# A hand-ordered opening and w_out sample rows by raw weights, in a layer of a hybrid attention encoder

## The chip, the cores and the metric

The kernel runs on one core of a Trainium2 chip. A core has five engines with a queue of instructions each: TensorE (PE, matrix products and transposes, results in PSUM), VectorE (DVE), ScalarE (ACT), GpSimd (POOL) and SyncE (SP, which here only issues DMA transfers). PEld is the loading of PE's stationary operand. An engine runs its instructions in the order in which they were put down; semaphores tie the engines together. The metric is the device time of one execution in microseconds, and the median over several executions is compared.

## The reference

One layer (DEPTH = 1) for two groups of rows that share the weights: 1024 prompt rows and 32 sample rows, with D_MODEL = 1024. All data are float32.

```python
ada = silu(c) @ w_ada + b_ada            # six vectors of 1024 per group
h   = rms_norm(x, g_pre_mix) * (1 + scale1) + shift1
p   = h @ w_in                           # 4256 columns: q latent, kv latent, rope key,
                                         # stick-breaking q, k, v, gate A, gate B
# branch A: latent attention, branch B: stick-breaking attention
merged = sigmoid(g_a) * (o_a @ w_proj_a) + sigmoid(g_b) * (o_b @ w_proj_b)
x  = x + gate1 * rms_norm(merged @ w_out, g_post_mix)
h2 = rms_norm(x, g_pre_ffn) * (1 + scale2) + shift2
x  = x + gate2 * rms_norm(conv_ffn(h2), g_post_ffn)
```

The change touches the first lines (ada for shift1 and scale1, the norm, the first columns of `p`) and the sample rows of `merged @ w_out`.

## The kernel before

A float32 product is made of three matmuls in a faster type: each operand is split into a high part, which is the value rounded by ScalarE (`hi`, line 68), and a low part, the difference, which VectorE makes (`lo`, line 71). `mm3` (lines 75 to 77) adds high x high, low x high and high x low in PSUM. Activations lie transposed, with the model's columns in the 128 partitions (eight blocks k = 0 to 7) and the 1056 rows (1024 prompt, 32 sample) along the free axis. PSUM has eight banks of 512 float32 columns, in rings by tag: `s` three, `mm` two, `tr` two, `pv` one. Most engines' orders come from a scheduler that goes by the order of the program text and by estimated durations. Blocks under `manual_schedule` keep the order of the text on the engines that they name.

**The opening** is `stage_h` (line 372). `ada_prep` makes silu(c), turned. `ada_half(hf)` (line 276) fetches eight chunks of `w_ada`, each 128 rows by the half `hf` of the columns of shift1 and of scale1 (512 KB), and adds their products with `cT`; the sum is copied (line 290), turned by two transposes (line 293), and given its bias (line 296) and the norm's gain (`gain`, line 272). Half 0 serves blocks k = 0 to 3, half 1 blocks 4 to 7. A row tile of 128 prompt rows is loaded, squared and summed by ScalarE (line 116), scaled by its rstd from GpSimd (lines 108, 109) on VectorE (line 385). `norm_T` (line 302) transposes it in PE (line 320) and lets ScalarE read PSUM, with scale and shift of ada in the same activation (line 326); so a turned tile stays in PSUM until ada's half is known. VectorE then makes the high part (line 329, or ScalarE for rows 512 on) and the low part (line 330). Rows 512 on also stay in `fq` as float32, for sums that a later product scheme needs.

SP issues in the opening: four row tiles, eight chunks, one `w_in` tile, four row tiles, a second `w_in` tile, eight chunks.

**`stage_qkv`** (line 443) then multiplies three column tiles of `w_in` of 128 columns by `mtile` (line 415): q pair 0 (line 660), k pair 0 (line 673), and a latent tile (line 678). Each takes three blocks of 352 rows, eight k and three matmuls, 72 in all. The k tile is transposed back and stored (line 485). Then pairs of column tiles follow by a scheme with seven products instead of eight (`pair`, line 596); it needs sums of the activations T1 to T4, made by `sums` (line 564) from `fq` and the split rows on VectorE and ScalarE, and sums of weights (lines 608 to 613), which are split in their turn (`half`).

**`stage_merge`** (line 2067) goes over eight blocks m of merged columns: a `w_proj_a` tile is loaded into the ring `wr` of two buffers (line 1910) and split, its 36 matmuls are gated, and the merged block is split (`mh`, `ml`). A row block of `w_out` is loaded into the same ring (line 2119) and split. `natural` (line 1988) multiplies the merged blocks with `w_out` in groups: m = 0 and 1 after the products of m = 2, m = 2 and 3 in two parts at m = 4 and 6, the rest at the end. The sample rows go by `natural_s` (line 2020): 32 columns as stationary operand, the high and then the low part of `w_out` streamed as float32, four quarters of 256 columns side by side. It is called for two, four and two blocks with an eviction each time (line 2032 adds).

Of the kernel before, what the change touches and what calls it, by code (L numbers as in the profile page):

```python
# [44 lines left out]
class K:  # L45
# [224 lines left out]
    def gain(self, out, v, g0, k0=0, n=8):  # L270
        k = slice(k0, k0 + n)
        self.nc.vector.scalar_tensor_tensor(
            out[:, k], self.adaT[:, v, k], 1.0, self.gvT[:, g0 + k0 : g0 + k0 + n].unsqueeze(2).broadcast_to([P, n, 2]),
            ALU.add, ALU.mult)

    def ada_half(self, hf, wp, tp):

        nc, a = self.nc, self.a
        acc = self.tl(tp, [P, 256], F32, f"ada{hf}")
        ps = self.bank("s")  # L280
        for k in range(KT):

            last = hf == 1 and k >= KT - 2
            w = self.tl(*((self.W, [P, 1024]) if last else (wp, [P, 2 * 512])), F32, "wr").rearrange("p (v n) -> p v n", v=2)
            nc.sync.dma_start(w, a["w_ada"][0, k * P : (k + 1) * P].rearrange("p (v h n) -> p v h n", v=6, h=2)[:, 0:2, hf])
            for j in range(4):
                c = (j % 2) * 256
                nc.tensor.matmul(ps[32 * j : 32 * j + 32, :256], self.cT[:, k], w[:, j // 2, c : c + 256],
                                 start=k == 0, stop=k == KT - 1)
        nc.vector.tensor_copy(acc, ps[:, :256])  # L290
        tr = self.bank("s")
        for c in range(2):
            nc.tensor.transpose(tr[:, c * P : c * P + P], acc[:, c * P : c * P + P], self.idt)
        for c in range(2):
            k = slice(4 * hf + c, 4 * hf + 4, 2)
            nc.vector.tensor_tensor(self.adaT[:, 0:2, k],
                                    tr[:, c * P : c * P + P].rearrange("p (v j r) -> p v j r", v=2, j=2)[:, :, :, 0:2],
                                    self.bT[:, :, k].unsqueeze(3).broadcast_to([P, 2, 2, 2]), ALU.add)
        self.gain(self.g1, 1, 0, 4 * hf, 4)


    def norm_T(self, t0, xs, g, sv, tp, k0=0, k1=KT):


        nc = self.nc
        if t0 < 8:
            n = len(xs) * P
            m = 512 // n
            c = slice(t0 * P, t0 * P + n)
            for k in range(k0, k1, m):  # L310
                tr = self.bank("tr")
                if t0:
                    f = self.fq[:, k : k + m, :n]
                else:
                    f = self.tl(tp, [P, 512], F32, "hf").rearrange("p (k c) -> p k c", k=m)
                for e in range(m):
                    kc = slice((k + e) * P, (k + e) * P + P)
                    for j, x in enumerate(xs):
                        o = e * n + j * P
                        nc.tensor.transpose(tr[:, o : o + P], x[:, kc], self.idt)  # L320
                h, l = self.Hht[:, k : k + m, c], self.Hlt[:, k : k + m, c]

                both = t0 == 4 and k0 == 0
                for e in range(m):
                    for x in (f, h) if both else (f,):
                        nc.scalar.activation(x[:, e], tr[:, e * n : e * n + n], AF.Identity,
                                             bias=self.adaT[:, sv, k + e, 0:1], scale=g[:, k + e, 0:1])
                if not both:
                    nc.vector.tensor_copy(h, f)
                nc.vector.tensor_tensor(l, f, h.bitcast(F32), ALU.subtract)  # L330
        else:
            tr = self.bank("tr")
            for c in range(2):
                nc.tensor.transpose(tr[:, c * P : c * P + P], xs[0][:, c * P : c * P + P], self.idt)
            f = self.fq[:, :, 512:]
            for k in range(k0, k1):
                j, c = k // 2, k % 2
                nc.scalar.activation(f[:, k], tr[:, c * P + 32 * j : c * P + 32 * j + 32],
                                     AF.Identity, bias=self.adaT[:, sv, k, 1:2], scale=g[:, k, 1:2])
            f, h, l = (x[:, k0:k1] for x in (f, self.Hht[:, :, TP:T], self.Hlt[:, :, TP:T]))  # L340
            nc.vector.tensor_copy(h, f)
            self.lo(l, f, h)
# [10 lines left out]
    def rstd_s(self, f, tp):  # L353
# [5 lines left out]
        ps = self.bank("tr")  # L359
# [12 lines left out]
    def stage_h(self):  # L372
        nc = self.nc
        self.new_H()
        a = self.a
        self.Fq = self.tc.alloc_tile_pool(name="fq", bufs=1, reuse_waits="tile")
        self.fq = self.Fq.tile([P, KT, TP - 512 + TS], F32, name="fq")
        with self.tc.tile_pool(name="st_h", bufs=2, reuse_waits="tile") as tp, self.tc.tile_pool(name="wada", bufs=8, reuse_waits="tile") as wp:
            self.ada_prep(tp)
            xts = []  # L380

            def load(t):
                x = self.tl(wp, [P, D], F32, "x")
                nc.sync.dma_start(x, a["x_prompt"][0, t * P : (t + 1) * P])
                nc.vector.tensor_scalar(x, x, self.rstd(self.sumsq(x, P, tp, "jk0", 1024), D, P), None, ALU.mult)
                xts.append(x)

            def norm(t, hf):
                self.norm_T(t, xts[t : t + 4] if t < 8 else [xs], self.g1, 0, tp, 4 * hf, 4 * hf + 4)

            for t in range(4):
                load(t)
            self.ada_half(0, wp, tp)
            norm(0, 0)
            w = [self.w_in_tile(672)]
            mk = self.tl(tp, [P, 272], F32, "mk")
            nc.gpsimd.dma_start(mk, a["k_mask"][:, P:])
            nc.vector.tensor_copy(self.msk, mk)
            for t in range(4, 8):
                load(t)  # L400
            w.append(self.w_in_tile(672 + 512))
            self.in_w = w
            norm(4, 0)
            xs = self.tl(tp, [P, 256], F32, "xs")
            self.quarters(xs, a["x_sample"][0], nc.gpsimd)
            nc.gpsimd.dma_start(self.sel, a["k_sel"])
            self.ada_half(1, wp, tp)
            nc.vector.tensor_scalar(xs, xs, self.rstd_s(xs, tp), None, ALU.mult)
            norm(0, 1)
            norm(8, 0)  # L410
            norm(4, 1)
            norm(8, 1)
# [30 lines left out]
    def stage_qkv(self):  # L443
# [6 lines left out]
        T4, T3, T1, T2 = ([Tp.tile([P, 4, HC], F32R, name=self.nm("T")) for _ in range(2)] for _ in range(4))  # L450
# [208 lines left out]
        wh, wl = self.w_in_tile(672)  # L659
        for c0, n, ps in self.mtile(wh, wl, self.Hh, self.Hl, self.BLK, KT):  # L660
# [8 lines left out]

        next(S)  # L670
        kf, lf = S0, Q0
# [6 lines left out]
        for c0, n, ps in self.mtile(wh, wl, self.Hh, self.Hl, self.BLK, KT, "mm mm pv"):  # L678
# [17 lines left out]
        Tp.release()  # L696

# [1322 lines left out]
    def natural_s(self, facc, lhs, ws, first, done=None):  # L2020

        nc = self.nc
        ps = self.bank("pv")
        mm = [(x, w) for x, wl in zip(lhs, ws) for w in wl]
        for i, (x, w) in enumerate(mm):
            for j in range(4):
                nc.tensor.matmul(ps[32 * j : 32 * j + 32, :256], x, w[:, j * 256 : j * 256 + 256],
                                 start=i == 0, stop=i == len(mm) - 1)
        if first:
            nc.scalar.copy(facc[8], ps[:, :256])  # L2030
        else:
            nc.vector.tensor_tensor(facc[8], facc[8], ps[:, :256], ALU.add)
        if done:
            done(8)
# [32 lines left out]
    def stage_merge(self):  # L2067
# [7 lines left out]
        lhs, lhs_s, ws = [], [], []  # L2075

        def drop(n):
            del lhs[:n], lhs_s[:n], ws[:n]

        def nat_s(n, first=False, done=None):  # L2080
            b = lambda x: x.bitcast(F32)
            self.natural_s(facc, lhs_s[:n], [(b(h), b(l)) for h, l in ws[:n]], first, done)

        def nat(n, first=False, done=None):
            if not done:
# [734 lines left out]
```

## Time and profile before

| | |
|---|---|
| median of 3 runs | 1675.18 us (1669.10 to 1675.49) |
| the profiled execution | 1672.13 us, its span 1670.4 us |
| granted TensorE clock | 0.997 of full speed |
| PE busy | 1631.8 us, 98% |
| DVE, ACT, POOL busy | 1239.5, 930.3, 290.9 us |
| DMA | 260.63 MB, 156 GB/s in the mean |

The span runs from the first to the last instruction in the trace. Matmuls overlap, so the time from one start to the next is the price of one, not its own duration. In rows of a timeline come first the start and the busy time of a group, then engine, line, operation, what is written from what, and a count; in brackets the idle time ahead of it and what ended it. In rows of stretches come the stretch, its length, busy time and count for PE, PEld, DVE, ACT and POOL (for one line only those engines that it has), then the granted clock, the DMA share and GB/s. Records of float32 matmuls count two to an instruction where the text says so.

### The profile page before, as it was taken

What the parts mean: (1) busy time and instruction counts of PE and PEld (TensorE: products, weight loads), DVE (VectorE), ACT (ScalarE), POOL (GpSimd) and SP (SyncE); (2) the same over time, 40 slices, a digit from 0 to 9 for tenths busy, and PEclk for the clock granted to TensorE, in tenths of its full rate; (3) what the DMA queues carried; (4) which work ended last, traced back from release to release, by engine and by line L of the source; (5) the groups of instructions that cost most, each with busy time, mean ns of one, the idle gap of its engine ahead of it and who ended that gap; (6) DMA issues with size and microseconds to landing.
All of it is one profiled execution on the core that took longest, in us unless ns stands there. A gap on an engine that the chain in (4) does not pass through costs nothing. (4 is left out here: it accounts for less than half of the span.)

```text
span 1670.4 us, 30244 instructions
## 1 busy us (share of the span) xinstructions
PE 1631.8 (98%) x11664; PEld 1496.5 (90%) x11664; DVE 1239.5 (74%) x2059; ACT 930.3 (56%) x1779; POOL 290.9 (17%) x568
## 2 busy tenths in 40 slices
PE   5999999999999999999999999999999999999998
PEld 3999999999998889998988799999999999877886
DVE  4865549888863689887766789878777777788456
ACT  5545337666654589887762675444444444544442
POOL 2113201211230221110000212211112112110013
PEclk9999999999999999999999999999999999999999
DMA  9345549777642532322374423333333333697643
GB/s 337 102 128 191 174 129 270 229 215 220 179 137 54 171 107 80 86 89 63 133 255 131 171 93 125 128 128 102 128 119 110 133 109 119 233 331 242 219 146 123
DMA packets 193857, 260.63 MB, mean 156 GB/s; under 512 B 23182, under 2 KB 132112, under 8 KB 193648
## 3 DMA queue, kind: packets, MB, share of 16 engines
q1 hardware_dynamic: 172944, 198.50, 38.5%
q0 software_dynamic: 20400, 59.56, 10.1%
q8 instruction: 92, 1.51, 0.4%
q10 hardware_dynamic: 368, 0.63, 0.1%
q14 instruction: 53, 0.43, 0.1%
HBM read 191.11 MB, written 67.82 MB: 155 GB/s over the span
## 5 line engine op out<-in xcount | busy, mean ns | idle before, releaser
L68 ACT ACTIVATE wh<-wr 128x512 fp32r<-128x512 f32 (+2 forms) x157 | 131.4, 839 | 226.7 <-PE s L2268 84.4
L71 DVE TENSOR_TENSOR wl<-wr,wh 128x512 fp32r<-128x512 f32 (+2 forms) x157 | 149.2, 954 | 86.0 <-ACT wh L68 85.8
L2267 PE MATMUL mm<-T,wh 128*128 128x256 f32 (+1 forms) x448 | 128.7, 288 | 0.0
L2269 PE MATMUL mm<-T,wl 128*128 128x256 f32 (+1 forms) x448 | 127.6, 285 | 0.4 <-DVE wl L71 0.2
L2268 PE MATMUL mm<-T,wh 128*128 128x256 f32 (+1 forms) x448 | 127.1, 284 | 0.0
L71 DVE TENSOR_TENSOR wl<-S,wh 128x1024 fp32r<-128x1024 f32 (+1 forms) x64 | 65.3, 1023 | 60.8 <-ACT wh L68 60.0
L75 PE MATMUL mm<-hh,wh 128*128 128x352 f32 x312 | 105.4, 338 | 0.0
L77 PE MATMUL mm<-hh,wl 128*128 128x352 f32 x312 | 101.9, 327 | 1.2 <-DVE wl L71 1.2
L76 PE MATMUL mm<-hl,wh 128*128 128x352 f32 x312 | 102.6, 329 | 0.4 <-DVE hl L330 0.4
L2269 PE MATMUL s<-T,wl 128*128 128x256 f32 (+1 forms) x360 | 102.6, 285 | 0.0
L2267 PE MATMUL s<-T,wh 128*128 128x256 f32 (+1 forms) x360 | 102.6, 285 | 0.0
L2268 PE MATMUL s<-T,wh 128*128 128x256 f32 (+1 forms) x360 | 102.2, 284 | 0.0
L845 PE MATMUL tr<-c,A 128*128 128x128 f32 x576 | 87.7, 273 | 1.1 <-ACT A L1011 0.9
L68 ACT ACTIVATE wh<-S 128x1024 fp32r<-128x1024 f32 (+1 forms) x64 | 57.4, 900 | 56.0 <-PE pv L2268 14.0
L2408 DVE SCALAR_TENSOR_TENSOR u<-u,c,u 128x1058 f32<-128x1058 f32 x68 | 87.0, 1317 | 2.0 <-ACT u L2405 0.7
L2267 PEld LDWEIGHTS mm<-T,wh 128*128 128x128 f32 x448 | 84.4, 188 | 1.4 <-ACT wh L68 1.2
L2269 PEld LDWEIGHTS mm<-T,wl 128*128 128x128 f32 x448 | 84.4, 189 | 1.1 <-DVE wl L71 1.1
L2268 PEld LDWEIGHTS mm<-T,wh 128*128 128x128 f32 x448 | 84.3, 188 | 0.0
L68 ACT ACTIVATE PTh<-tr 128x512 fp32r<-128x512 f32 x96 | 57.6, 601 | 36.8 <-PE tr L845 30.6
L2267 PE MATMUL tr<-T,wh 128*128 128x272 f32 (+1 forms) x272 | 77.8, 286 | 0.0
L2269 PE MATMUL tr<-T,wl 128*128 128x272 f32 (+1 forms) x272 | 77.7, 286 | 0.1
L2268 PE MATMUL tr<-T,wh 128*128 128x272 f32 (+1 forms) x272 | 77.3, 284 | 0.0
(773 smaller groups left out, 5738.9 us busy)
## 6 DMA issues: line engine op xcount, KB each, us to landing
wr<-in_w_up_dram SPq DMA_DIRECT2D x44, 512.0 KB, 4.0
dr<-in_w_down_dram SPq DMA_DIRECT2D x43, 512.0 KB, 5.5
wr<-in_w_in_dram SPq DMA_DIRECT2D x33, 512.0 KB, 4.8
A<-in_w_ada_dram SPq DMA_DIRECT2D x32, 512.0 KB, 6.6
wr<-gdn SPq DMA_DIRECT2D x30, 512.0 KB, 4.6
gdn<-u POOLq DMA_DIRECT2D x23, 512.0 KB, 5.2
t<-gd SPq DMA_DIRECT2D x16, 528.0 KB, 5.5
wr<-in_w_ada_dram SPq DMA_DIRECT2D x16, 512.0 KB, 9.3
```

Source lines behind the costliest of these rows:

```text
L68: self.nc.scalar.activation(out, in_, AF.Identity, scale=scale)
L71: return self.nc.vector.tensor_tensor(out, full, hi.bitcast(F32), ALU.subtract)
L75: m(ps, lh, rh, start=start, stop=False)
L76: m(ps, lh, rl, start=False, stop=False)
L77: self.pe = m(ps, ll, rh, start=False, stop=stop).ins
L845: self.nc.tensor.transpose(tr[:, (2 * s + q) * P : (2 * s + q + 1) * P], at[q][:, b * P : b * P + P], self.idt)
L2267: m(ps[:, :n], w[0][:, k], x[0][:, k, c], start=first and k == 0, stop=False, skip_group_check=True)
L2268: m(ps[:, :n], w[0][:, k], x[1][:, k, c], start=False, stop=False, skip_group_check=True)
L2269: i = m(ps[:, :n], w[1][:, k], x[0][:, k, c], start=False, stop=k == 3, skip_group_check=True)
L2408: nc.vector.scalar_tensor_tensor(y, u[:, w : w + YW], self.cvT[:, w, cc : cc + 1], y, ALU.mult, ALU.add)
```

## The change

*The opening.* One list, `OPENING`, gives the order of PE, ScalarE and VectorE. Its tokens: `V` products of an ada chunk; `C`, `F`, `G` copy, turn and finish of half 0 or 1; `q`, `s` square and scale of a row tile; `l`, `h` four transposes of its low or high four blocks into a named bank; `c` the copy of that bank to SBUF by ScalarE; `H`, `f` the norm's scale and shift, as high part or in float32 in place, by ScalarE (`A`), VectorE (`D`) or a cast (`c`); `L` the low part; `S` the sample rows; `M`, `N` the products of a block k with the high (four matmuls) and low (two) part of the activations, for q and k tile at once, over row blocks of 512, 256 and 288; `i`, `o` halves of a `w_in` tile's split; `w` transposes of the identity that are not used. Row tiles are scaled by rstd and turned before ada is known; the ada part comes from SBUF afterwards. A square now takes epsilon by a column of its own that GpSimd writes. The chunks of half 0 come first on SP, with row tiles between them. The latent `w_in` tile is loaded and split here too, into the two tiles of T1, which are allocated in the opening.

*`w_out` sample rows.* One bank collects all eight blocks; each block's raw `w_out` rows are streamed once, an iteration after they were loaded.

```diff
+    OPENING = (
+        "V0 V1 V2 V3 q0 w8 V4 s0 q1 w9 h0.K1 l0.K2 ch0.A.K1 V5 cl0.A.K2 s1 q2 w8 l1.Q1 h1.Q2 cl1.A.Q1 i00 w4 V6 s2 "
...
+        "V13 H11.A f32.D M01 L01 i11 L32 N02 N01 f11.A H21.D M11 o11 H31.A V14 M12 L11 f22.A f21.D N12 f31.A V15 L21 "
+        "N11 M21 C1 L31 F1 H22.c N21 i20 M31 G1 i21 M22 L22 H40.A N31 S1 N22 M32 H43.A N32 H50.D M40 f40.A o21 f50.A "
+        "M41 L40 M42 f43.A L50 N40 H53.A L43 M50 f63.A H60.D N42 H73.D N50 f53.A H63.c M60 f73.A L53 M52 f60.A L63 N52 "
+        "L73 H70.A N41 M51 L60 N51 f70.A M61 o20 N61 N60 L70 M70 N70 M71 M62 N62 M72 N72 N71 "
+    )
...
+    def norm_part(self, xT, k, part):
+
+        c0, c1 = ((0, 512), (512, 768), (768, 1024), (512, 1024))[part]
+        v = self.fq[:, k, c0 - 512 : c1 - 512] if part else xT[:, k]
+        return v, self.Hht[:, k, c0:c1], self.Hlt[:, k, c0:c1], self.adaT[:, 0, k, 0:1], self.g1[:, k, 0:1]
+
+    def norm_from(self, engine, dst, *which):
+        v, h, _, b, g = self.norm_part(*which)
+        o = h if dst == "H" else v
+        if engine == "c":
+            self.nc.vector.tensor_copy(h, v)
+        elif engine == "D":
+            self.nc.vector.tensor_scalar(o, v, g, b, ALU.mult, ALU.add)
         else:
...
+            self.nc.scalar.activation(o, v, AF.Identity, bias=b, scale=g)
...
+        self.T1p = self.tc.alloc_tile_pool(name="sum1", bufs=1, side="right", reuse_waits="tile")
+        self.T1 = [self.T1p.tile([P, 4, HC], F32R, name=self.nm("T")) for _ in range(2)]
...
+            def warm(n):
+                for _ in range(n):
+                    nc.tensor.transpose(bk[0][:, :P], self.idt, self.idt)
...
+            hl.append([x.rearrange("p k c -> p (k c)")[:, :1024] for x in self.T1])
+            with self.tc.manual_schedule(engines={E.PE, E.Activation, E.DVE}):
...
+                fetch(0, 1, 2, 3)
+                load(0)
+                fetch(4)
+                load(1)
+                fetch(5)
+                load(2)
+                weights(0, 0, 4)
...
+                        if i == 1:
+                            fetch(6)
+                            load(3)
+                            weights(1, 0, 4)
+                            fetch(7)
+                            load(4)
...
+                        elif i == 7:
+                            fetch(8, 9, 10, 11)
+                            weights(0, 4, 8)
+                            weights(1, 4, 8)
+                            fetch(12, 13)
...
+                        if turned[t] == 2:
+                            if t < 3:
+                                load(t + 5)
+                            elif t == 3:
+                                fetch(14)
+                            elif t == 4:
+                                fetch(15)
+                                weights(2, 0, 8)
...
-        wh, wl = self.w_in_tile(672)
-        for c0, n, ps in self.mtile(wh, wl, self.Hh, self.Hl, self.BLK, KT):
+        banks, (wh, wl) = self.begun
+        for (c0, n), ps in zip(self.XB, banks["q"]):
...
-        wh, wl = self.w_in_tile(672 + 512)
-        for c0, n, ps in self.mtile(wh, wl, self.Hh, self.Hl, self.BLK, KT, "s"):
-            nc.scalar.copy(kf[:, c0 : c0 + n], ps[:, :n])
...
-        wh, wl = self.w_in_tile(2 * P)
...
-    def natural_s(self, facc, lhs, ws, first, done=None):
-
-        nc = self.nc
-        ps = self.bank("pv")
-        mm = [(x, w) for x, wl in zip(lhs, ws) for w in wl]
-        for i, (x, w) in enumerate(mm):
...
+    def natural_s(self, m, x, w):
+
+        if m == 0:
+            self.os = self.bank("pv")
+        for j in range(4):
+            self.nc.tensor.matmul(self.os[32 * j : 32 * j + 32, :256], x, w[:, j * 256 : j * 256 + 256],
+                                  start=m == 0, stop=m == KT - 1, skip_group_check=True)
...
+        def sample():
+            self.natural_s(*rows.pop(0))
+
+        def sample_out():
+            sample()
+            nc.scalar.copy(facc[8], self.os[:, :256])
+            done(8)
...
             raw = self.tl(self.W, [P, D], F32, "wr")
             nc.sync.dma_start(raw, a["w_out"][0, mc])
             ws.append(self.dsplit(E3, raw, "dh dl" if m % 4 < 3 else "dr dr"))
+            if rows:
+                sample()
+            rows.append((m, ms, raw))
```

More of the change, by code (lines that the diff above doesn't have):

```diff
@@ L271, in gain @@
         k = slice(k0, k0 + n)
-        self.nc.vector.scalar_tensor_tensor(
+        return self.nc.vector.scalar_tensor_tensor(
             out[:, k], self.adaT[:, v, k], 1.0, self.gvT[:, g0 + k0 : g0 + k0 + n].unsqueeze(2).broadcast_to([P, n, 2]),
-            ALU.add, ALU.mult)
-    def ada_half(self, hf, wp, tp):
-        nc, a = self.nc, self.a
-        acc = self.tl(tp, [P, 256], F32, f"ada{hf}")
[L280 to L291, printed above, removed]
-        for c in range(2):
[L293 to L299, printed above, removed]
@@ L302, in norm_T @@
-    def norm_T(self, t0, xs, g, sv, tp, k0=0, k1=KT):
-        nc = self.nc
[L306 to L330, printed above, removed]
-        else:
[L332 to L342, printed above, removed]
@@ new lines, in ada_copy, with ada_turned, rest @@
+    def ada_copy(self, hf, ps, tp):
+        acc = self.tl(tp, [P, 256], F32, f"ada{hf}")
+        self.nc.vector.tensor_copy(acc, ps[:, :256])
+        return acc
+    def ada_turned(self, hf, acc, tr):
+        for c in range(2):
+            self.nc.tensor.transpose(tr[:, c * P : c * P + P], acc[:, c * P : c * P + P], self.idt)
+        def rest():
+            for c in range(2):
+                k = slice(4 * hf + c, 4 * hf + 4, 2)
+                self.nc.vector.tensor_tensor(self.adaT[:, 0:2, k],
+                                             tr[:, c * P : c * P + P].rearrange("p (v j r) -> p v j r", v=2, j=2)[:, :, :, 0:2],
+                                             self.bT[:, :, k].unsqueeze(3).broadcast_to([P, 2, 2, 2]), ALU.add)
+            self.gain(self.g1, 1, 0, 4 * hf, 4)
+        return rest
@@ new lines, in norm_lo, with norm_sample @@
+    def norm_lo(self, *which):
+        v, h, l, _, _ = self.norm_part(*which)
+        self.lo(l, v, h)
+    def norm_sample(self, k):
+        nc, ada, g, add = self.nc, self.adaT, self.g1, self.nc.vector.tensor_tensor
+        ks, cols = slice(k, k + 4), lambda x: x.broadcast_to([P, 4, TS])
+        f, h, l = self.fq[:, ks, 512:], self.Hht[:, ks, TP:T], self.Hlt[:, ks, TP:T]
+        add(f, f, cols(g[:, ks, 1:2]), ALU.mult)
+        add(f, f, cols(ada[:, 0, ks, 1:2]), ALU.add)
+        nc.vector.tensor_copy(h, f)
+        self.lo(l, f, h)
@@ L386, in load @@
[L386 to L400, printed above, removed]
@@ new lines, in scale, with turn, put @@
+            def scale(t):
+                x = xs[t]
+                nc.vector.tensor_scalar(x[:, :D], x[:, :D], rs.pop(t), None, ALU.mult)
+            def turn(t, hf, tr):
+                for e in range(4):
+                    k = 4 * hf + e
+                    nc.tensor.transpose(tr[:, e * P : e * P + P], xs[t][:, k * P : k * P + P], self.idt)
+            def put(t, hf, tr, engine):
+                dst, c = (xT, t) if t < 4 else (self.fq, t - 4)
+                copy = nc.scalar.copy if engine == "A" else nc.vector.tensor_copy
+                copy(dst[:, 4 * hf : 4 * hf + 4, c * P : c * P + P], tr.rearrange("p (e c) -> p e c", e=4))
@@ new lines, in stage_h, with weights, split @@
+            kc = lambda x: x.rearrange("p (k c) -> p k c", k=8)
+            def weights(i, k0, k1):
+                c0 = (672, 1184, 256)[i]
+                k = slice(k0, k1)
+                nc.sync.dma_start(kc(raws[i])[:, k], a["w_in"][0, k0 * P : k1 * P, c0 : c0 + P].rearrange("(k p) c -> p k c", p=P))
+            def split(i, hf, low):
+                raw, (h, l) = raws[i], hl[i]
+                c = slice(512 * hf, 512 * hf + 512)
+                if low:
+                    self.lo(l[:, c], raw[:, c], h[:, c])
+                else:
+                    self.hi(h[:, c], raw[:, c])
@@ new lines, in products @@
+            def products(k, b, low):
+                c0, n = self.XB[b]
+                x, m = (self.Hl if low else self.Hh)[k][:, c0 : c0 + n], nc.tensor.matmul
+                for i, bank in ((0, bq[b]), (1, bk[b])):
+                    wh, wl = (kc(y)[:, k] for y in hl[i])
+                    if low:
+                        m(bank[:, :n], wh, x, start=False, stop=k == KT - 1)
+                    else:
+                        m(bank[:, :n], wh, x, start=k == 0, stop=False)
+                        m(bank[:, :n], wl, x, start=False, stop=False)
@@ L2018, in natural @@
                     sample()
-    def natural_s(self, facc, lhs, ws, first, done=None):
-        nc = self.nc
-        ps = self.bank("pv")
-        mm = [(x, w) for x, wl in zip(lhs, ws) for w in wl]
-        for i, (x, w) in enumerate(mm):
[L2026 to L2034, printed above, removed]
+    def natural_s(self, m, x, w):
+        if m == 0:
+            self.os = self.bank("pv")
+        for j in range(4):
+            self.nc.tensor.matmul(self.os[32 * j : 32 * j + 32, :256], x, w[:, j * 256 : j * 256 + 256],
+                                  start=m == 0, stop=m == KT - 1, skip_group_check=True)
     def new_facc(self, pool):
@@ L2074, in stage_merge @@
         xh, xl = self.xh, self.xl
[L2075 removed]
+        lhs, ws, rows = [], [], []
         def drop(n):
[L2078 to L2082, printed above, removed]
+            del lhs[:n], ws[:n]
+        def sample():
[4 more added lines that the diff above has]
+            done(8)
         def nat(n, first=False, done=None):
[L2085 to L2087 removed]
+            self.natural(facc, lhs[:n], ws[:n], first, done, sample_out)
             drop(n)
```

122 lines of the change are left out of this document (95 added, 27 removed), and 4 rows, old and new, of the table OPENING.

## The prediction

> **What bounds the kernel now.** First the page and the busy time of the engines by stretch.
>
> ```profile
> span 1670.4 us, 30244 instructions
> PE 1631.8 (98%) x11664; PEld 1496.5 (90%) x11664; DVE 1239.5 (74%) x2059; ACT 930.3 (56%) x1779; POOL 290.9 (17%) x568
> ```
> ```profile
> 0.00:45.20 45.20, 26.69 (x198) 14.22 (x198) 19.65 (x45) 20.88 (x34) 12.35 (x28) 0.92 0.88 312
> 56.90:90.95 34.05, 34.02 (x234) 33.69 (x233) 33.45 (x40) 19.78 (x35) 6.87 (x12) 1.00 0.40 129
> 90.95:200.00 109.05, 109.05 (x904) 108.69 (x903) 60.17 (x106) 46.93 (x106) 29.82 (x49) 1.00 0.54 173
> ```
>
> TensorE (PE) is idle for 38.6 us of the span, and 18.5 of these lie before 45.2 us. From there on PE has no gaps, so what PE need not do after 45.2 us leaves the span, as long as nothing else becomes late. The second row warns: VectorE (DVE) is busy for 33.45 of its 34.05 us, so it runs beside PE with hardly any spare time.
>
> The DMA view of the first 45 us (40 slices of 1.125 us) shows what fills the opening, and one stretch its clock (third number from the end):
>
> ```profile
> GB/s 0 58 325 381 376 369 289 308 379 373 402 395 399 386 386 386 390 373 314 346 399 408 411 388 331 314 374 388 386 386 379 390 390 384 388 138 25 0 0 0
> DMA packets 8018, 14.08 MB, mean 313 GB/s; under 512 B 568, under 2 KB 2784, under 8 KB 8016
> ```
> ```profile
> 28.00:34.00 6.00, 4.63 (x16) 3.12 (x14) 4.72 (x8) 4.93 (x10) 3.51 (x7) 0.50 1.07 368
> ```
>
> The 14 MB stream without a pause until slice 36, about 40 us. The last chunk of w_ada therefore lands near 40, and yet PE multiplies it late:
>
> ```profile
> 43.16 1.50 PE L288 MATMUL s<-wr,cT 128*32 128x256 f32 x24
> 45.21 0.44 PE L293 MATMUL s<-c,ada 128*128 128x128 f32 x2 [0.55 <-DVE ada L290]
> 69.03 1.29 PE L485 MATMUL tr<-c,S 128*128 128x128 f32 x8
> 70.07 0.41 PE L77 MATMUL mm<-hh,wl 128*128 128x352 f32 x1
> 81.34 0.32 PE L77 MATMUL pv<-hh,wl 128*128 128x352 f32 x1
> 81.50 0.28 PE L2267 MATMUL mm<-hh,wh 128*128 128x256 f32 x1
> ```
> ```profile
> 20.00:45.20 25.20, 3.51 (x8) 1.90 (x8) 0.86 0.84 295
> 45.20:81.50 36.30, 20.45 (x64) 11.84 (x64) 1.00 0.37 117
> ```
>
> The second fence counts line 75, the first of the three matmuls of a step: 8 before 45.2, 64 after. So 24 of the 216 matmuls of the first three column tiles (q pair 0, k pair 0, the latent tile) are done by 45.2 us and 192 are not. They go at 81.50 - 81.34 = 0.16 us each, which is 30.9 us; 32 transposes of row tiles at 0.13 (the 69.03 row: 1.04 for eight) and those of the k tile nearly fill the 36.3 us to 81.5, where the first pair begins.
>
> **The change, part 1: the opening.** The traffic is the same 14 MB ahead of the last chunk (the third w_in tile now follows it), so by the GB/s row it still lands at about 40.2. Transposes no longer wait for ada: a row tile is scaled, turned, copied, and normalised from SBUF. On SP the loads of row tiles 5 to 7 and of chunks 14 and 15 now wait for turned tiles, and the later chunks stand behind them; by the GB/s row the tiles that they wait for land some 10 us before the transfer's turn, and a square, a scaling and eight transposes take about 4 us, so I cost it at nothing; past that cover each us costs one. GpSimd gets eight memsets and loses eight scalings beside this. Durations:
>
> ```profile
> L385 DVE TENSOR_SCALAR x<-x,rs 128x1024 f32<-128x1024 f32 x8 | 5.9, 751 | 4.6 <-POOL rs L109 4.4
> L329 DVE CAST hh<-fq 128x512 fp32r<-128x512 f32 x4 | 1.6, 422 | 0.1
> L116 ACT ACTIVATE jk<-x 128x1024 f32<-128x1024 f32 x8 | 8.4, 1052 | 4.9 <-DMA x<-in_x_prompt_dram 4.9
> L326 ACT ACTIVATE fq<-tr,c,c 128x512 f32<-128x512 f32 x8 | 6.2, 785 | 1.4 <-PE tr L320 1.2
> ```
>
> Between the eighth chunk (7.2 MB in the new order, about 21.5 us) and the sixteenth the list gives ScalarE (ACT) ten PSUM copies, four squares, the equivalent of 6.5 activations of 512 columns and two weight halves. With the copy and the activation at 0.6 to 0.67 and the square at 1.15 that is 16 us, in 18.7. PE gets there 40 transposes (5.2), 13 fillers (1.7), eight chunks at 0.5 (the x24 row) and products of the first four blocks of rows (8.4), 19.3 us in 18.7: no slack. I put the end of the last chunk's products at 41.3, 1.1 after landing. The copies and the normalisations from SBUF are forms that before lacks; I bound them by the 422 ns cast and the 785 ns activation and take ACT's at the latter's end, DVE's (one input, one output) near the 751 ns for 1024 columns, so 0.4 for 512.
>
> After that point PE has: the list's left-over products of blocks 1 to 3, 3.2 us at 0.46 ns a column (0.16 for 352); the two transposes of the turn, 0.4; the products of blocks 4 to 7, 11.7; the latent tile, 72 x 0.16 = 11.6; the k transposes, 1.1. That is 28.0 us. The 3.2 cover the way from the last product to the first normalised block (a copy 0.4, the turn 0.44, three short DVE steps, one activation 0.79), and ACT's 12 passes of 512 (8 us) and DVE's 11 us run beside the 11.7. PE reaches the first pair at 41.3 + 28.0 = 69.3 instead of 81.5: **12.2 us** for PE alone.
>
> DVE doesn't gain as much. Its last opening instruction and the ones that the first pair waits for are
>
> ```profile
> 56.53 0.28 DVE L71 TENSOR_TENSOR hl<-fq,hh 128x128 fp32r<-128x128 f32 x1
> 68.36 1.21 DVE L71 TENSOR_TENSOR wl<-wr,wh 128x1024 fp32r<-128x1024 f32 x1
> 82.46 0.69 DVE L71 TENSOR_TENSOR wl<-S,wh 128x512 fp32r<-128x512 f32 x1
> 88.46 1.28 DVE L71 TENSOR_TENSOR wl<-wr,wh 128x512 fp32r<-128x512 f32 x2
> 89.66 1.25 DVE L71 TENSOR_TENSOR T<-fq,T 128x1056 fp32r<-128x1056 f32 x1
> ```
> ```profile
> 87.34 0.28 PE L2267 MATMUL mm<-T,wh 128*128 128x256 f32 x1
> 93.19 0.28 PE L2267 MATMUL mm<-T,wh 128*128 128x256 f32 x1
> 96.12 0.28 PE L2267 MATMUL mm<-T,wh 128*128 128x256 f32 x1
> ```
>
> The low half of the pair's second weights ends at 83.1 and PE wants it at 87.3 (4.2 to spare); the third ends at 89.7 for 93.2 (3.5); T4 at 90.9 for 96.1 or, in its second block, 1.4 later (6.6). In the new list DVE has 11 us after the last chunk (eight low parts at 0.64, the 88.46 row below, five passes at 0.4, two weight halves, the sample rows, 256-column parts), so it leaves the opening at about 53.0 rather than 56.8, and the latent tile's low half (1.14, the 68.36 row) is done by then, while the mask's cast adds 0.2: it comes forward by 4.8. If DVE's order stays, PE stalls for 12.2 - 4.8 - 3.5 = 3.9; if T4 moves behind the weights, for 12.2 - 4.8 - 6.6 = 0.8. Both orders come from the same program text, so I take 3.0, nearer the first. T1's halves now hold the latent weights and can be written only from 69.3 on; two activations and two differences end at about 73, ahead of their use at 78: hidden. The copies of q and k tile move to after a common end and stand beside the latent tile. Part 1: 12.2 - 3.0 = **9.2 us**.
>
> **Part 2: sample rows by raw weights.** The high and low rows go, one pass over the raw tile stays:
>
> ```profile
> 906.76 0.64 PE L2027 MATMUL pv<-dh,gs 128*32 128x256 f32 x8
> ...
> 908.63 0.43 PE L75 MATMUL mm<-QH,wh 128*128 128x352 f32 x1
> ```
> ```profile
> 905.00:912.00 7.00, 1.93 (x32) 0.94 (x32) 1.00 0.25 79
> ```
> ```profile
> L2027 PE MATMUL pv<-dh,gs x48: 379/379/404, 834.9 to 925.9; 128*32 128x256 f32 x48
> L2027 PE MATMUL pv<-dl,gs x48: 379/379/403, 835.4 to 926.4; 128*32 128x256 f32 x48
> L2027 PE MATMUL pv<-dr,gs x32: 379/379/379, 907.6 to 927.2; 128*32 128x256 f32 x32
> ```
>
> Here 32 records take 1.87 us, 0.058 each; 128 take 7.5. Of these 64 go, 3.7 us; they now come in eight places rather than five, each with some 0.1 of change-over, so I take -3.5. The evictions that vanish are off the path. But the raw tile is now held until the sample rows of the iteration after have been multiplied, and its ring has two buffers, which w_proj_a shares:
>
> ```profile
> 848.36 0.38 SPq L1910 DMA_DIRECT2D wr<-in_w_proj_a_dram  x1
> ```
> ```profile
> L68 ACT ACTIVATE wh<-wr x8: 617/640/1060, 826.2 to 920.0; 128x512 fp32r<-128x512 f32 x6, 128x1024 fp32r<-128x1024 f32 x2
> L71 DVE TENSOR_TENSOR wl<-wr,wh x8: 683/688/1227, 826.8 to 929.4; 128x512 fp32r<-128x512 f32 x6, 128x1024 fp32r<-128x1024 f32 x2
> DMA to landing us min/median/max: 3.5/4.4/6.9
> ```
> ```profile
> 867.02 0.32 PE L75 MATMUL mm<-QH,wh 128*128 128x352 f32 x1
> 872.84 0.39 PE L75 MATMUL s<-dh,mh 128*128 128x512 f32 x1
> ```
>
> The fifth w_proj_a tile (m = 4) was issued at 848.4 and multiplied from 867.0. Now the other buffer holds a w_out tile whose sample rows stand behind the products of m = 3, which end at 867.0. Issue, landing, high and low part (0.38 + 4.4 + 0.64 + 0.69) make 6.1 us, on PE's path unless the w_out products (48 of 512 columns x 0.46 ns = 11.3 us, from 872.84 on) come first. The same holds for m = 5, 6 and 7: at most 24.4, at least 0. Behind the blocked load on SP stand the gate loads of the same iteration, which want it no sooner. For m = 5 and 7 the w_out products stand in between by the program; for m = 4 and 6 they must be drawn forward, and the first waits for the last merged row. I take 3.0 in all, nearer the end where they fill. Part 2: **-0.5 us**.
>
> **Sum.** 9.2 + 0.5 = 9.7. The profiled execution took 1672.1 (span 1670.4 and 1.7 around it), which gives 1662.4. The median of the runs shown, 1675.2, is 3.1 above it; by that it is 1665.5. I forecast 1665.
>
> **A rule against it.** In the 28 to 34 row PE was granted half its clock. The list has 58 filler transposes to avoid that. The Trainium skill, "TensorE: Matmul & The Clock Gate", Part 4 (PE-mode transpose), says that transposes don't count as busy for the clock. No row of before has transposes alone. By it the sum would be that of the first rival below, by the 0.86 the one above.
>
> **Rivals.**
> - *Half clock.* The fillers don't keep PE awake (for: the 0.50 row; against: the mean of 0.86 over 20 to 45.2, in the row of line 75, leaves all but some 7 us at full clock, though PE did mostly transposes and small matmuls there). Each 6 us at half clock costs 3 of PE's work, which had nothing to spare: with 12 us so, the last chunk is 6 late, gain 3.7: 1671.5. Chance 0.15.
> - *The list stalls.* In-order engines and loads that wait for turned tiles delay the last chunk by 4 us or more; the opening doesn't do what it says. Gain 5 or less: 1671. Chance 0.17.
> - *No cap.* DVE's order moves T4 back and the w_out products fill every gap: 12.2 - 0.8 + 3.5 = 14.9, 1660. Chance 0.13.
> - *Slower: the ring.* The four w_proj_a loads are all waited for: 24.4 - 3.5 - 9.2 = 11.7 above before, 1687. It decides once over 12.7 + 8.4 of the 24.4 are not filled. For: a two-buffer ring; against: 22.6 us of w_out products can fill. Chance 0.07.
>
> The forecast has 0.48; by itself it is 1660 to 1670. A measurement of this kernel tells 0.5%, 8.4 us, from no change. Of the forecast somewhat over three fifths (0.31) lies beyond it, with the third rival 0.13 and little of the first two (0.06): faster 0.50. Slower is most of the ring and a bit of stalls, 0.08; the rest 0.42. The range takes in the third rival's gain and a ring half filled: 1656 to 1677.
>
> **What would show it.** Right: the last chunk's products end near 41 (each us later is one lost); clock 1.00 throughout; the first pair starts near 69 with DVE waits of 1 to 4 us in it; 64 records on the sample rows, and gaps of about 3 us ahead of the products of m = 4 and 6. Wrong: a first pair later than 74, or PE idle above 10 us in the merge.

## The result, and the profile after

The changed kernel took 1664.59 us (median of 7 runs, 1662.04 to 1667.81) beside 1673.79 for the kernel before (median of 7, 1669.10 to 1677.73): a ratio of 0.9946, 95% interval 0.9928 to 0.9964. That is 9.2 us, and the forecast was 1665 with a sum of 9.7. The gain sits on the 0.5% that a measurement can tell. The total hides two errors that cancel: the opening brought less than its 9.2 us, the rows of the merge more than their 0.5. That the sum came out so close is luck.

The page of the kernel after, its span and engines:

```profile
span 1660.3 us, 30265 instructions
PE 1631.4 (98%) x11664; PEld 1496.5 (90%) x11664; DVE 1242.7 (75%) x2075; ACT 937.7 (56%) x1792; POOL 290.1 (17%) x568
```

PE is as busy as before (1631.4 to 1631.8), so the whole gain is idle time gone: 28.9 us left of 38.6. The 66 filler transposes are in that busy time. The opening by stretch, cut at the ends of the eighth and the sixteenth chunk's products and at the first pair (columns: stretch, its length, busy time and instructions of PE, PEld, DVE, ACT, POOL, granted clock, DMA share, GB/s):

```profile
0.00:27.10 27.10, 16.43 (x148) 11.55 (x148) 7.98 (x24) 10.65 (x20) 7.01 (x23) 1.00 0.93 328
27.10:47.80 20.70, 20.60 (x170) 14.28 (x166) 15.34 (x38) 17.30 (x32) 3.40 (x5) 1.00 1.01 328
47.80:75.47 27.67, 27.67 (x181) 26.36 (x182) 26.98 (x46) 20.17 (x35) 4.26 (x7) 1.00 0.26 95
```

PE's timeline after, at the eighth chunk, the first products, the sixteenth chunk and the first pair:

```profile
26.50 0.64 PE L286 MATMUL tr<-wr,cT 128*32 128x256 f32 x8
...
29.57 0.50 PE L458 MATMUL mm<-hh,wh 128*128 128x512 f32 x1
...
47.15 0.64 PE L286 MATMUL tr<-x,cT 128*32 128x256 f32 x8
...
75.47 0.28 PE L2394 MATMUL mm<-hh,wh 128*128 128x256 f32 x1
```

PE has almost no gap from 27 us on, and the clock is 1.00 in all three stretches. The first pair starts at 75.47, 6.0 us earlier than before and 6.2 later than the forecast's 69.3. All of that lateness stands already at the sixteenth chunk: its products end at 47.8, not at 41.3.

VectorE after, at the end of the opening and ahead of the pair, and the matmul that uses that low part (one row of DVE's timeline for the end of the opening, one for the low part, one of PE's):

```profile
58.85 0.29 DVE L543 CAST c<-x 128x272 bf16<-128x272 f32 x1
...
74.95 0.69 DVE L71 TENSOR_TENSOR wl<-wr,wh 128x512 fp32r<-128x512 f32 x1
...
75.95 0.29 PE L2396 MATMUL mm<-hh,wl 128*128 128x256 f32 x1
```

And the same step of VectorE before, both low halves together:

```profile
74.14 1.28 DVE L71 TENSOR_TENSOR wl<-wr,wh 128x512 fp32r<-128x512 f32 x2
```

Before, both halves were done at 75.42, 6.1 us ahead of the pair at 81.50. After, the first is done at 75.64 and wanted at 75.95. The 6.0 us that PE gained were taken out of VectorE's lead, and 0.3 us of it is left: the pair starts with no wait, yet PE could hardly have come earlier by itself.

In the merge after, the sample rows of the first two tiles, the load of the fifth w_proj_a tile (m = 4), and its first product; below them all the waits of PE between 800 and 935 us:

```profile
826.59 0.64 PE L2157 MATMUL pv<-wr,gs 128*32 128x256 f32 x8
827.16 0.43 PE L76 MATMUL mm<-QL,wh 128*128 128x352 f32 x1
...
859.21 0.40 SPq L2042 DMA_DIRECT2D wr<-in_w_proj_a_dram  x1
...
862.97 0.32 PE L75 MATMUL mm<-QH,wh 128*128 128x352 f32 x1
```
```profile
PE tr L371 <- ACT hf L369: 0.6, 2, 0.4
PE s L75 <- DVE facc L2146: 0.6, 1, 0.6
PE s L75 <- ACT mh L68: 0.4, 1, 0.4
PE tr L2362 <- DVE f L2291: 0.3, 1, 0.3
```

One place of eight records takes 827.16 - 826.59 = 0.57 us, so the eight places take 4.6. The load for m = 4 is issued 10.9 us later than before (848.36), although the merge itself begins 6.6 us earlier. The prediction had this delay. But no wait stands ahead of its products: none of the four rows names the low or high part of a w_proj_a tile.

### The profile page after: what moved, and what is told of

Its sections match the earlier page's. It is cut to its first block, busy times and chain, and to the rows that moved or that the text cites. A ratio compares the mean times of both kernels' runs of the same rounds, so it can differ in the third digit from the quotient of the medians.

```text
span 1660.3 us, 30265 instructions
## 1 busy us (share of the span) xinstructions
PE 1631.4 (98%) x11664; PEld 1496.5 (90%) x11664; DVE 1242.7 (75%) x2075; ACT 937.7 (56%) x1792; POOL 290.1 (17%) x568
## 3 DMA queue, kind: packets, MB, share of 16 engines
q0 software_dynamic: 20400, 59.56, 10.2%
## 5 line engine op out<-in xcount | busy, mean ns | idle before, releaser
L68 ACT ACTIVATE wh<-wr 128x512 fp32r<-128x512 f32 (+3 forms) x158 | 130.9, 831 | 211.6 <-PE s L2395 86.2
L71 DVE TENSOR_TENSOR wl<-wr,wh 128x512 fp32r<-128x512 f32 (+3 forms) x158 | 148.5, 943 | 86.0 <-ACT wh L68 85.5
L75 PE MATMUL mm<-hh,wh 128*128 128x352 f32 x272 | 91.4, 336 | 0.0
L77 PE MATMUL mm<-hh,wl 128*128 128x352 f32 x272 | 87.9, 323 | 1.2 <-DVE wl L71 1.2
L76 PE MATMUL mm<-hl,wh 128*128 128x352 f32 x272 | 87.8, 323 | 0.0
```

The lines of the kernel that those rows point to most:

```text
L68: self.nc.scalar.activation(out, in_, AF.Identity, scale=scale)
L71: return self.nc.vector.tensor_tensor(out, full, hi.bitcast(F32), ALU.subtract)
L75: m(ps, lh, rh, start=start, stop=False)
L76: m(ps, lh, rl, start=False, stop=False)
L77: self.pe = m(ps, ll, rh, start=False, stop=stop).ins
```

## The experiments

Each ratio is against the kernel before on the same chip in the same set of runs; it need not equal the quotient of two medians.

| run | median, us | ratio, 95% interval |
|---|---|---|
| opening alone | 1665.83 | 0.9957 (0.9944 to 0.9969) |
| sample rows alone | 1670.76 | 0.9987 (0.9978 to 0.9996) |
| no fillers | 1662.25 | 0.9936 (0.9924 to 0.9948) |
| no fillers, sample rows scaled first | 1662.73 | 0.9938 (0.9925 to 0.9951) |
| half the latent tile | 1663.28 | 0.9941 (0.9924 to 0.9959) |
| own ring for w_proj_a, four gate buffers | 1673.25 | 1.0000 (0.9991 to 1.0009) |
| changed kernel again | 1665.28 | 0.9950 (0.9936 to 0.9965) |
| no fillers, sample first, four copies on DVE | 1660.27 | 0.9920 (0.9905 to 0.9935) |
| shared ring, four gate buffers | 1672.96 | 1.0002 (0.9992 to 1.0012) |
| no fillers, sample first, four copies on DVE, then 29 fillers in the gaps | 1660.65 | 0.9936 (0.9923 to 0.9950) |

**The two parts one at a time.** The first run is the changed kernel with `natural_s` and the merge loop of before; the second is the kernel before with those two of after:

```diff
-    def natural_s(self, m, x, w):                          # raw rows, one tile
+    def natural_s(self, facc, lhs, ws, first, done=None):  # high and low rows
...
-            if rows:
-                sample()
-            rows.append((m, ms, raw))
+            lhs_s.append(ms)
```

> The changed kernel with the w_out sample rows of before. Theory A (the split that the profile after suggests): the opening is worth the 6.0 us by which the first pair starts earlier (75.5 against 81.5), so 6 to 6.5 us below before, ratio 0.996, and the sample rows take 128 records again. Theory B (the split of the prediction): the opening is worth 9.2, ratio 0.9945, and the rows nearly nothing.

> The kernel of before with the w_out sample rows by raw weights alone. Theory A: 3.5 to 4 us below before, ratio 0.9978, no PE wait on a w_proj_a load in the merge. Theory B (the prediction's term): loads behind the held buffer cost 3 us of it, 0.5 us below before, ratio 0.9997, with gaps of PE of some 1.5 us at m = 4 and 6.

The opening alone is worth 7.1 us (1672.95 - 1665.83; by the interval 5.2 to 9.4), with its first pair at 75.31 us. The rows alone are worth 2.2 (0.7 to 3.7), which lies between the two theories. They add up to 9.3, beside 9.2 for the changed kernel here and 8.1 in a later set (1673.34 - 1665.28). With intervals of some 2 us either way that shows no dependence between the parts and excludes none.

**The fillers.** The list loses its `w` steps (58 transposes), and `warm(8)` ahead of it goes too, 66 in all; in the second run the sample rows' reciprocal root and scaling also move ahead of the first chunk, and their turn behind the second:

```diff
-    "V0 V1 V2 V3 q0 w8 V4 s0 q1 w9 h0.K1 ...
+    "V0 V1 V2 V3 q0 V4 s0 q1 h0.K1 ...
-                warm(8)
+                ys = self.rstd_s(y, tp, R[1])              # second run only
+                nc.vector.tensor_scalar(y, y, ys, None, ALU.mult)
```

> The changed kernel with no filler transposes (58 fewer, nothing else). Theory A: PE runs behind its own list up to the first products (29.6 us), and 9 us of the 18.6 before are fillers; without them the sixteenth chunk's products end 2 to 5 us earlier than 47.8 at a clock of 1.00. Theory B (the half clock): PE then idles in front of its waits, the granted clock falls to 0.50 in some stretch between 20 and 48 us as it did from 28 to 34 in before, and the first pair starts later than 75.5.

> The changed kernel without fillers, and with the sample rows' square, sum, rstd and scaling ahead of the first chunk's products and their turn behind the second's (in the change the first row tile's rstd and scaling stand behind these on GpSimd and VectorE and end at 18.4 instead of 14 us). Theory A: the first row tile is scaled at 14 to 15 us, the later loads of row tiles leave earlier, and the sixteenth chunk's products end 4 to 7 us before 47.8; of this at most 1 to 2 us reach the end, since VectorE is then late in the first pair: PE waits of 2 to 5 us for its low parts between 65 and 95 us. Theory B (no cap by VectorE): the whole gain at the sixteenth chunk is found again at the end.

Without fillers, by stretch, and at the eighth chunk, the sixteenth chunk and the first pair:

```profile
16.00:20.00 4.00, 2.82 (x29) 1.93 (x26) 1.75 (x3) 1.61 (x3) 0.41 (x2) 1.00 1.06 367
20.00:24.00 4.00, 2.61 (x28) 1.31 (x26) 1.54 (x3) 4.00 (x10) 1.29 (x4) 1.00 1.07 394
24.00:28.00 4.00, 2.19 (x14) 1.73 (x14) 3.25 (x9) 3.20 (x7) 0.60 (x1) 1.00 1.02 395
```
```profile
23.00 0.64 PE L286 MATMUL tr<-wr,cT 128*32 128x256 f32 x8
...
44.73 0.64 PE L286 MATMUL tr<-x,cT 128*32 128x256 f32 x8
...
73.05 0.28 PE L2393 MATMUL mm<-hh,wh 128*128 128x256 f32 x1
```

The eighth chunk comes at 23.00 instead of 26.50, but the sixteenth only 2.4 us earlier (44.73 instead of 47.15), and 2.4 us reach the pair: PE now waits for scaled row tiles and for the first normalised rows, idle for 4.4 of 16 to 28 us. VectorE moves with it, since the list ties its steps to the same chunks, and no wait follows the pair. In this execution the clock stayed at 1.00 with PE busy for 2.2 of 4 us. Scaling the sample rows first changes hardly anything more: the sixteenth chunk comes at 44.42, not 4 to 7 us earlier than in the changed kernel, and the first pair at 72.73. Both stand about 1 permille below the changed kernel, within the intervals.

**Is VectorE a cap?** The changed kernel with only half of the latent tile's sum, which takes 5.8 us from PE between the opening and the pair and nothing from VectorE:

```diff
-for c0, n, ps in self.mtile(wh, wl, self.Hh, self.Hl, self.BLK, KT, "tr mm pv"):
+for c0, n, ps in self.mtile(wh, wl, self.Hh, self.Hl, self.BLK, 4, "tr mm pv"):
```

> Leaves out half of the latent tile's products (blocks of rows 4 to 7 of its sum), so the output is not the reference's: 36 matmuls of 352 columns less, 5.8 us less work for PE between the opening and the first pair, and nothing less for DVE. PE reaches the first pair at 75.5 - 5.8 = 69.7 us, which is the forecast's 69.3. Theory (DVE is the cap): DVE is busy without a gap from 59 to 96 us and finishes the low part of the pair's second weights at 80.4, when PE now wants it at 81.3; so PE waits 4.9 us there, about 1 more at the low part of T4, and nearly all of the 5.8 is lost: 0 to -1.5 us against the changed kernel's 1664.6. Rival (no cap, DVE's order gives way): no wait of PE above 1 us in 60 to 130 us and -5.8 us, 1658.8.

PE's timeline from the first pair on, and VectorE's at the same step:

```profile
69.20 0.28 PE L2394 MATMUL mm<-hh,wh 128*128 128x256 f32 x1
...
75.18 0.39 PE L2396 MATMUL mm<-hh,wl 128*128 128x256 f32 x1 [4.84 <-DVE wl L71]
```
```profile
74.44 0.68 DVE L71 TENSOR_TENSOR wl<-wr,wh 128x512 fp32r<-128x512 f32 x1
```

PE is at the pair at 69.20, the forecast's 69.3, and then stands 4.84 us for the low part of the pair's first weights, which VectorE finishes at 75.12. The size is what was expected; the place is one step earlier (the first weights, not the second). No other wait follows up to 130 us. But after the wait PE was granted only 0.55 of its clock for 3.8 us, which costs it another 1.7 us. That stretch, and the first product with `T`, here and in the changed kernel:

```profile
75.18:79.00 3.82, 3.82 (x19) 3.82 (x19) 3.82 (x5) 0.89 (x2) 0.00 (x0) 0.55 0.06 18
```
```profile
81.67 0.28 PE L2394 MATMUL mm<-T,wh 128*128 128x256 f32 x1
```
```profile
81.31 0.28 PE L2394 MATMUL mm<-T,wh 128*128 128x256 f32 x1
```

So in this execution nothing of the 5.8 us is left at 81.67: 4.84 went to VectorE and the rest to the clock. The medians differ by 2.0 us (1665.28 - 1663.28), with intervals that overlap. VectorE is the cap for PE by itself.

**The shared ring.** The changed kernel with two buffers of their own for w_proj_a, paid for with one of the five gate buffers; then, as a control, the shared ring with four gate buffers:

```diff
-BUFS = {..., "t": 5, ...}
+BUFS = {..., "t": 4, ...}                                  # both runs
-self.split_proj(self.w_proj_a(m) ...)
+self.split_proj(self.w_proj_a(m, self.tl(E3, [P, 512], F32, "wa")) ...)   # first run only
```

> The changed kernel, with a ring of its own for the w_proj_a tiles of the merge (two buffers of 512 columns; the space is from the ring of gate rows, four buffers rather than five), so that they no longer wait for the raw w_out tile. If the shared ring costs nothing, as the absence of PE waits ahead of the products of m = 4 to 7 says: within 1 us of the changed kernel. If the ring is why 3.7 us of matmuls saved on the sample rows moved the end of the merge by 0.4 to 1.7 us only: 1.5 to 3 us faster, w_proj_a for m = 4 issued near 848 again rather than at 859. If the fifth gate buffer mattered: slower, with waits on the gate rows.

> The control for the run with a ring of its own for w_proj_a, which took 1673.3: the changed kernel with four gate-row buffers rather than five and the shared ring as it was. If the shared ring costs nothing, this one is as slow as that one, 1672 to 1675, and the fifth gate buffer is worth 8 us. If the shared ring costs something, it is slower than that one by as much, above 1675. If the own ring itself did the harm, it stays near 1665.

The load of m = 4 on SP, with its own ring and with the shared one:

```profile
842.21 0.43 SPq L2042 DMA_DIRECT2D wa<-in_w_proj_a_dram  x1
```
```profile
864.35 0.40 SPq L2042 DMA_DIRECT2D wr<-in_w_proj_a_dram  x1
```

The load comes 22 us earlier and the time is the same: 1673.25 and 1672.96. So with four gate buffers the shared ring costs nothing within about 2 us; with five, no wait of the result names a w_proj_a tile. What both runs lost is the fifth gate buffer, 8 us. Part of it is in the merge. PE's longest waits between 780 and 940 us, first with the own ring, then with the shared one (columns: in all, times, longest):

```profile
PE s L75 <- ACT mh L68: 1.5, 1, 1.5
PE pv L2157 <- DVE gs L2240: 1.5, 1, 1.5
```
```profile
PE pv L2157 <- DVE gs L2240: 1.5, 1, 1.5
PE s L75 <- ACT mh L68: 1.4, 1, 1.4
```

In the changed kernel the wait for `mh` is 0.4 us and the one for `gs` is not there. More of it is in the stage after the merge, between 940 and 1100 us:

```profile
PE tr L2348 <- DVE t L2327: 2.2, 1, 2.2
PE tr L2348 <- ACT t L68: 1.8, 2, 1.0
```
```profile
PE tr L2348 <- DVE t L2327: 2.2, 1, 2.2
PE tr L2348 <- ACT t L68: 1.9, 2, 1.0
```

They wait for the same tiles `t`, which the second normalisation takes from the gate buffers; the changed kernel's longest wait there is 0.4 us. In 825 to 860 and 940 to 1000 us PE is busy for 3.2 and 4.3 us less with the own ring than in the changed kernel (31.4 to 34.6, 54.7 to 59.0), which makes up nearly all of the 8.

**A faster list.** Four PSUM copies of row tiles 0 and 1 move from ACT, which is full in 20 to 24 us, to DVE; the fillers are left out and the sample rows scaled first. The last run puts 29 fillers back where PE waited:

```diff
-... ch0.A.K1 V5 cl0.A.K2 s1 q2 w8 l1.Q1 h1.Q2 cl1.A.Q1 i00 w4 V6 s2 ch1.A.Q2 ...
+... ch0.D.K1 V5 cl0.D.K2 s1 q2 l1.Q1 h1.Q2 cl1.D.Q1 i00 V6 s2 ch1.D.Q2 ...
+... V5 w7 ... V6 w7 ... V7 w7 ... H10.D w8 M00 ...         # last run only
```

> The changed kernel unaltered, beside the next one on the same chip: 0.9946 of the kernel before, first pair at 75.5 us.

> The changed kernel without its 66 filler transposes, the sample rows scaled ahead of the first chunk, and four PSUM copies of row tiles 0 and 1 moved from ACT to DVE, which is busy only 1.5 of 4 us in 20 to 24 us while ACT is full. If PE's start of dense work sets the end: first pair at 72 to 72.7 and 2.5 to 3 us faster than the changed kernel. If the fillers kept the clock up, a half-speed stretch shows in 12 to 30 us and the gain is gone. If DVE holds PE back after the pair, the first pair comes earlier, with a wait on a low part after it.

> The kernel without fillers, with sample rows first and four copies on DVE, with 29 fillers back, put only where PE waited 0.9 to 1.2 us (ahead of the transposes of row tiles 1, 2 and 3 and of the first products), so that they fit into the waits. Theory (the fillers keep the clock, their number is what cost PE): granted clock 1.00 in 24 to 32 us, where it was 0.63 without them, first pair at 72.5 to 73.5, 1658 to 1660. If they are not needed: the same as without, 1660.3. If a transpose does not keep the clock: a half-speed stretch in 24 to 32 us again.

By stretch, first without fillers, then with 29 of them in the gaps:

```profile
24.00:28.00 4.00, 1.85 (x11) 1.53 (x12) 3.10 (x9) 2.95 (x7) 0.72 (x2) 0.94 1.03 398
28.00:32.00 4.00, 4.00 (x17) 3.33 (x17) 4.00 (x7) 3.92 (x7) 1.64 (x2) 0.63 1.05 387
```
```profile
24.00:28.00 4.00, 3.68 (x29) 3.07 (x26) 2.50 (x8) 2.86 (x5) 0.55 (x1) 1.00 1.02 400
28.00:32.00 4.00, 3.90 (x27) 2.68 (x27) 3.97 (x8) 3.92 (x7) 1.65 (x2) 1.00 1.05 385
```

Without fillers the profiled execution ran part of 24 to 32 us at reduced clock (0.63 of full speed in 28 to 32), after a stretch in which PE was busy for 1.85 of 4 us. Its first pair stood at 74.73. With the 29 fillers the clock is 1.00 and the pair starts here:

```profile
72.86 0.28 PE L2392 MATMUL mm<-hh,wh 128*128 128x256 f32 x1
```

Of the 1.9 us between the two pairs, 0.6 stood before the clock fell (the first products start at 27.52 and 26.95), so in these two executions the reduced clock goes with some 1.3 us. The medians of the two, 1660.27 and 1660.65, don't differ. The expectation had the gain gone if a half-speed stretch showed, and it is not. Beside the changed kernel (1665.28 in the set of the first, ratio 0.9950) the version without fillers took 5.0 us less, and the two intervals just part (0.9935 and 0.9936). It beats both kernels, but where the 5.0 us come from is not shown: in its profiled execution, one of the slower of six (1661.79), the pair is only 0.7 us earlier than in the changed kernel. Nor do the four copies show a gain of their own: the kernel without fillers and with the sample rows first, 0.9938 (0.9925 to 0.9951), overlaps with it, and its pair at 72.73 is as early as that with fillers in the gaps. The version with fillers in the gaps was not run beside the changed kernel.

## Why the prediction was right, and where its steps were wrong

**The end of the last chunk's products: 41.3 predicted, 47.8 measured.** This is the step that failed, and all of the 6.2 us at the pair stand there. The prediction took PE to be done with the eighth chunk right after landing, near 22 us; it ended at 27.1. The fillers ahead of it were costed at nothing. Their line alone, by stretch (busy time of PE, then PEld):

```profile
10.00:27.10 17.10, 8.03 (x53) 6.52 (x53) 1.00 1.00 364
27.10:47.80 20.70, 1.58 (x13) 1.45 (x13) 1.00 1.01 328
```

Fifty-three fillers took 8 us of the 17 before 27.1. Without them the eighth chunk came 3.5 earlier, which the run without fillers shows; in that run rows that are not yet scaled keep PE for the rest. The landing at about 21.5 was early, too: with the 29 fillers in the gaps PE waits 1.1 us for the eighth chunk itself, until 23.11. From the eighth to the sixteenth chunk the prediction had 19.3 us of work; it took 20.7. Late by 5.1 at the start and 1.4 on the way makes 6.5. Taking all fillers out gives back only 2.4 of them at the sixteenth chunk, since PE then waits in their place (4.4 us idle in 16 to 28). So the prediction missed two things: the price of the fillers, and PE's waits for scaled rows, which its sum does not have.

**The 28.0 us after it** were right: 75.47 - 47.8 = 27.7.

**VectorE's stall: 3.0 predicted, 0 measured.** The prediction had DVE leave the opening at about 53.0; it left at 59.1. Its 11 us of work after the last chunk were right (47.86, the copy of the last sums, to 59.1), they only began some 6 us later, too. PE and DVE were late by nearly the same (6.2 and 6.1), so the stall between them did not open. That VectorE limits the pair was right in kind: 0.3 us of slack after, and 4.84 us of waiting when PE alone came at 69.2. The prediction looked at the second and third weights; the low part of the first weights ends the wait.

**Part 1 in all: 9.2 predicted, 7.1 measured** (5.2 to 9.4: the interval just holds the 9.2, the place of the pair does not). The pair accounts for about 6 of it. The prediction had PE without gaps after 45.2 us, yet 20.1 of the 38.6 us of idle time lie behind that point. Among them are three waits in 780 to 940 us that the profile of before has and that of the opening alone lacks, 3.2 us in all:

```profile
PE s L75 <- ACT mh L68: 1.5, 1, 1.5
PE tr L845 <- ACT A L1011: 0.9, 1, 0.9
PE s L76 <- DVE QL L71: 0.8, 1, 0.8
```

The one for `QL` stands in the run with the own ring again (0.7 us), whose opening is the new one, and the one for `mh` is 0.4 us in the changed kernel. Against them, the profile of the opening alone was granted 0.50 of its clock in 581.6 to 584 us, where the changed kernel had 1.00. Whether the change removes the waits is open.

Could the 6 us at the pair be the clock's rather than the list's? Before, PE was at half clock in a part of the opening. The run with the rows alone has that same opening, and its slow stretch was longer (first before, then the rows alone):

```profile
27.37:34.20 6.83, 5.46 (x17) 3.75 (x17) 5.33 (x10) 5.56 (x11) 4.06 (x8) 0.50 1.07 364
```
```profile
23.94:34.18 10.24, 8.04 (x28) 6.18 (x28) 8.46 (x14) 8.52 (x16) 4.24 (x8) 0.50 1.06 376
```

Its pair started at 81.10, no later than the 81.50 of before. That speaks against the clock; no run shows the old opening at full clock.

**Part 2: 0.5 predicted, 2.2 measured** (0.7 to 3.7). The records that go were put at 3.5 us, and that was right: 128 x 0.058 and five change-overs of 0.1 are 8.0, the eight places take 4.6, which saves 3.4. The ring was put at 3.0 and cost nothing that could be found: the fifth load was late just as forecast, but from issue to products it took 3.8 us, not 6.1, and w_out products of 512 columns stood in front of it. The term belonged at its lower bound. Of the 3.4 some seem to come back as waits. PE in 830 to 940 us, first with the opening alone, then in the changed kernel:

```profile
830.00:940.00 110.00, 109.68 (x612) 90.56 (x611) 73.91 (x104) 52.81 (x78) 8.52 (x11) 1.00 0.57 187
```
```profile
830.00:940.00 110.00, 108.00 (x556) 87.61 (x555) 73.33 (x103) 53.80 (x80) 8.41 (x12) 1.00 0.57 190
```

PE idles 1.7 us more there, waiting for the last sums and their squares (the rows of waits in the result). It is one execution of each, and the interval of the rows holds 3.4 as well, so this much is argued rather than shown. The length of the merge also varies by itself. From the first `mm<-QH,wh` of the merge to the first `tr<-c,f` it took 118.9 us before, 115.4 with the rows alone, 117.3 with the opening alone, 117.0 and 118.3 in the two profiles of the changed kernel, and 115.6 to 115.7 with half the latent tile and with the last two lists, whose merge is the same code. So single profiles put the rows' worth anywhere from 3.5 us to nothing.

**The rivals.** *Half clock* did not come: 1.00 in every stretch of the opening. The rule that the Trainium skill gives in "TensorE: Matmul & The Clock Gate", Part 4 (PE-mode transpose), would have had the fillers do nothing for the clock. No run bears that out: between two kernels that differ in 29 filler transposes, the one without them was granted 0.63 in 28 to 32 us and the one with them 1.00. That is one execution of each, and the run without any filler and without the four copies kept 1.00 as well, so it does not prove that the fillers did it. *The list stalls* is what happened in part: the last chunk is 6.5 us late, which that rival had as 4 or more. By the run without fillers, 2.4 us of it are filler work; behind that stand waits for rows that the in-order engines have not yet scaled. Its 1671 was not reached, because VectorE's stall went with the lateness and the rows paid more. *No cap* fell with the run on half the latent tile. *The ring* fell with the two ring runs.

## What to carry to other kernels

In an in-order engine a filler is work like any other: price each at its duration unless a wait stands at that very place, and put it only there; here 8.0 us of fillers delayed the eighth chunk by 3.5. When one engine is brought forward, look at how far the next one was ahead at the point where they meet; here the 6 us gained were VectorE's lead, and only a change that moves both, as the run without fillers did, goes further. A buffer that was held longer cost nothing here, since the transfer that it delayed had other work in front of it, while a buffer taken from a ring that looks generous cost 8 us.

## What the runs showed of the hardware

The granted clock can fall without a long gap, and it need not. In the run without fillers, and in the one that has four copies on VectorE besides, PE did the same ahead of the first products: gaps of 1.0 and 1.2 us, and 1.4 us busy of 3.57 (first the former, then the latter):

```profile
23.61:27.18 3.57, 1.40 (x14) 1.06 (x11) 2.69 (x8) 2.77 (x6) 0.33 (x2) 1.00 1.02 400
```
```profile
23.95:27.52 3.57, 1.41 (x14) 1.06 (x10) 2.69 (x8) 2.52 (x6) 0.32 (x2) 1.00 1.02 397
```

In the 3.4 us after that the first was granted 1.00 and the second 0.50. Neither the length of the gaps nor the busy share tells the two apart, so a profile at full clock is no proof that the next execution has it. Apart from the one that ends the span, the half-clock stretches in these profiles are 3.4 us long or two or three times that (3.4 here, 6.8 and 10.2 in the old opening). In dense work one of 3.4 us costs about 1.7 us (an estimate: half of it), as much as some of the differences argued about above.
